# Half of a linear-attention merge on GpSimd, two small copies on ScalarE, and a head's mean one step later

## The chip, the cores and the metric

One core of a Trainium2 chip runs the whole program. The metric is the device time of one execution in microseconds; the kernel before was timed three times (2321.75, 2323.82 and 2325.22 us), and its median is 2323.82 us.

## What is computed

The reference is a two-layer encoder trunk over 16 meta tokens and 256 grid tokens (D = 2048), all in float32. Each layer projects the stream once, runs a gated linear attention (GLA, 4 heads, both directions) and a neighbourhood attention (NA, 16 heads) on parts of that projection, projects the concatenated outputs, normalises, and runs a squared-ReLU MLP. Cut to what matters here, one direction of the GLA is:

```python
bcum = jnp.cumsum(gi, axis=-2)
inter = jnp.einsum('bhtd,bhde->bhte', qi * jnp.exp(bcum), S)
decay = jnp.exp(jnp.where(incl, diff, -jnp.inf))
scores = jnp.einsum('bhtd,bhsd,bhtsd->bhts', qi, ki, decay)
intra = jnp.einsum('bhts,bhse->bhte', scores, vi)
...
o = o * lax.rsqrt(jnp.mean(jnp.square(o), axis=-1, keepdims=True) + LN_EPS) * norm_w
o = o.reshape(B, L, GLA_HEADS * GLA_DV) * jax.nn.silu(r)
```

The last two lines are where a head's mean comes in: a head's output is divided by its root mean square over 256 channels.

## The kernel before

**Weights.** The weights, 770 tiles of 512 KB, stream from HBM once, as 128x1024 tiles (`raw`, issued by SyncE at L195). Each tile is split by `halves` into a high part `wh`, a float32r copy made by ScalarE (ACT, L218), and a low part `wl` = raw - wh made by VectorE (DVE, L219). TensorE (PE) multiplies by both: a dense layer's output is high times high, high times low and low times high, accumulated in PSUM. `raw`, `wh` and `wl` have three buffers each (`wst`, bufs=3). One tile feeds 24 matmuls of 128x272 (L253), or 8 of width 512 and 8 of 256 where the two high terms go as one.

**Order of the work.** The program is written in the order of PE's dense products. After each weight tile `pump` runs steps of two queues of Python generators: `fg` (neighbourhood attention, evictions) and `bg` (the GLA heads). A step is what stands between two `yield`s. `pump` gives `fg` one step and `bg` 1.3 or 1.4 steps a tile (`GLA_R`, `GLA_NA`); a step after `yield True` is one that wants PE, and is held back for up to two tiles until it can go beside another such step. Before the last group of projections of a layer (`g == 5` in `layer`) what is left of `bg` is run to its end at one place. Within this order the recording layer may still move instructions of an engine past each other; each engine then works through its own list in order.

**A GLA head** (`gla_head`, L586 on) has these steps. Decays and the scaled keys and queries lie in `S`: `S[:, 0]` the keys' half, `S[:, 1]` the queries'. Seven levels of a tree double a block at each level: `gather` copies both into `U` (ACT, L606), `merge` multiplies one half of the blocks by the decay total of the neighbouring block, once for the keys' half (`odd` = 0) and once for the queries' (`odd` = 1) (DVE, L615), and then joins the totals in `dec` (GpSimd, called POOL, L617). `group` makes the level scores on PE (L629) and copies them into `A` and `Am` (L641 to L656). PE multiplies across the halves (L681, L686); ACT copies to `A` and `Am` (L692, L696); `stack` and `split` make float32r pairs `am` (L345, L346) and `parts` (L339, L340). The products with V follow (L716 to L720), then squares (ACT, L721), the gate (DVE, L723), their sum `rs` (`grs` in the profile, DVE, L725), the mean, and a Newton step for the inverse root (`newton`, L574 to L578), after which the outputs `y` are split.

**The mean** (`mean`, L975 on) splits `rs` into a pair `sp` (ACT L339, DVE L340), yields, and lets PE sum over the partitions by a matrix of ones (two matmuls, L983). The layer norms use the same helper, without a pool of their own.

**Keys and values of the neighbourhood attention** (`ev_na`): ACT copies the grid columns of a projection out of PSUM (L540), DVE the 16 meta columns, doubled, into a 128x32 strip (L541), POOL two overlaps (L544). Both copies read the PSUM bank `mm` that PE fills again four products later.

## Time and profile before

| what | value |
|---|---|
| median of three runs | 2323.82 us |
| the profiled execution: its own time / its span | 2323.91 us / 2322.1 us |
| PE busy | 2304.2 us (99%) |
| DVE busy | 1526.4 us (66%) |
| ACT busy | 1223.0 us (53%) |
| POOL busy | 155.4 us (7%) |
| mean granted TensorE clock | 0.999 |

The span runs from the first to the last instruction; the execution's own time is 1.8 us longer. Busy time of PE counts matmuls whose ends are modelled, so the places where PE stands still are read from its waits and from the order of time. The merges lie in two stretches, from 108 to about 280 us in layer 0 and from 1293 to 1459 us in layer 1; neighbourhood attention overlaps them, and its last products (L851) start at 1531 us in layer 1.

### The profile page before, as it was taken

How to read it: one execution, taken by the hardware profiler on the slowest of the kernel's cores; microseconds unless marked ns; L12 is line 12 of the kernel's file. 1: busy time of each engine (PE TensorE's matmuls, PEld its weight loads, DVE VectorE, ACT ScalarE, POOL GpSimd, SP SyncE). 2: the span in 40 equal slices, each digit the busy share in tenths (PEclk: the TensorE clock that was granted, in tenths of full speed). 3: DMA queues.
4: the chain of work that ended last, by engine and by line, in shares of the span. 5: the costliest groups of instructions: out<-in, count | busy, mean ns of one | idle time of the engine just before them, and what ended most of it. 6: DMA issues, size and time to landing. Idle time of an engine off the chain costs nothing.

```text
span 2322.1 us, 45272 instructions
## 1 busy us (share of the span) xinstructions
PE 2304.2 (99%) x18420; PEld 2188.9 (94%) x18420; DVE 1526.4 (66%) x2408; ACT 1223.0 (53%) x2096; POOL 155.4 (7%) x232
## 2 busy tenths in 40 slices
PE   9999999999999999999999999999999999999998
PEld 9999999999999999999999899889988888888888
DVE  5588878875544455547576788688866555666655
ACT  5666655564433344444456766655654334555443
POOL 0023210100000000000020122200100000000000
PEclk9999999999999999999999999999999999999999
DMA  8556666565555556665655556665666666667664
GB/s 259 155 164 184 199 189 177 173 181 181 182 181 178 179 181 182 180 179 178 182 173 173 173 175 209 195 187 181 198 191 196 194 191 193 192 196 218 195 195 150
DMA packets 129824, 431.65 MB, mean 186 GB/s; under 512 B 14792, under 2 KB 23496, under 8 KB 129616
## 3 DMA queue, kind: packets, MB, share of 16 engines
q1 hardware_dynamic: 127024, 421.95, 59.9%
q10 hardware_dynamic: 2592, 6.82, 0.8%
q8 instruction: 144, 2.36, 0.4%
q14 instruction: 64, 0.52, 0.1%
HBM read 420.32 MB, written 8.39 MB: 185 GB/s over the span
## 4 chain that ended last, share of the span: by engine, by line
PE 91%; DVE 5%; ACT 2%; issue 1%; DMA 1%; POOL 0%; DVEq 0%; ACTq 0%; SPq 0%
PE mm L253 53%; PE mm L265 29%; PE mm L304 4%; PE mm L314 2%; DVE wl L219 1%; PE bg L304 1%; ACT wh L218 1%; ACT ns L756 0%; DVE S L615 0%; PE bg L851 0%; PE bg L470 0%; PE bg L629 0%; DVE acc L1085 0%; POOL dec L617 0%; DMA raw<-in_wff 0%
## 5 line engine op out<-in xcount | busy, mean ns | idle before, releaser
L219 DVE TENSOR_TENSOR wl<-raw,wh 128x1024 fp32r<-128x1024 f32 (+1 forms) x770 | 935.9, 1223 | 621.8 <-ACT wh L218 518.5
L218 ACT CAST wh<-raw 128x1024 fp32r<-128x1024 f32 (+1 forms) x770 | 804.7, 1047 | 755.8 <-PE mm L253 352.6
L253 PE MATMUL mm<-x,wh 128*128 128x272 f32 (+3 forms) x4544 | 806.8, 294 | 0.0
L253 PEld LDWEIGHTS mm<-x,wh 128*128 128x128 f32 x4544 | 648.0, 188 | 15.5 <-issue 0.8
L253 PE MATMUL mm<-x,wl 128*128 128x272 f32 (+3 forms) x2432 | 520.6, 285 | 2.9 <-DVE wl L219 2.9
L253 PEld LDWEIGHTS mm<-x,wl 128*128 128x128 f32 x2432 | 391.4, 188 | 3.4 <-DVE wl L219 3.4
L253 PE MATMUL mm<-y,wh 128*128 128x272 f32 (+1 forms) x1440 | 235.0, 285 | 0.0
L253 PEld LDWEIGHTS mm<-y,wh 128*128 128x128 f32 x1440 | 199.7, 188 | 0.1
L265 PE MATMUL mm<-x,wh 128*128 128x512 f32 x832 | 193.8, 390 | 0.0
L265 PEld LDWEIGHTS mm<-x,wh 128*128 128x128 f32 x832 | 154.3, 188 | 31.0
L253 PE MATMUL mm<-u,wh 128*128 128x272 f32 (+1 forms) x1056 | 172.1, 285 | 0.0
L265 PE MATMUL mm<-y,wh 128*128 128x512 f32 x688 | 162.3, 389 | 0.0
L265 PEld LDWEIGHTS mm<-y,wh 128*128 128x128 f32 x688 | 128.7, 188 | 26.8 <-issue 0.4
L253 PE MATMUL mm<-y,wl 128*128 128x272 f32 (+1 forms) x720 | 146.5, 284 | 0.0
L253 PEld LDWEIGHTS mm<-u,wh 128*128 128x128 f32 x1056 | 146.3, 188 | 0.0
L265 PE MATMUL mm<-u,wh 128*128 128x512 f32 x496 | 118.3, 391 | 0.0
L253 PEld LDWEIGHTS mm<-y,wl 128*128 128x128 f32 x720 | 112.5, 188 | 0.0
L265 PEld LDWEIGHTS mm<-u,wh 128*128 128x128 f32 x496 | 90.9, 188 | 17.6
L253 PE MATMUL mm<-u,wl 128*128 128x272 f32 (+1 forms) x528 | 107.4, 284 | 0.0
L265 PEld LDWEIGHTS mm<-x,wl 128*128 128x128 f32 x832 | 98.5, 188 | 2.1
L265 PE MATMUL mm<-x,wl 128*128 128x256 f32 x832 | 99.0, 276 | 0.0
L265 PEld LDWEIGHTS mm<-y,wl 128*128 128x128 f32 x688 | 84.3, 188 | 2.8
(275 smaller groups left out, 2285.0 us busy)
## 6 DMA issues: line engine op xcount, KB each, us to landing
raw<-in_wff SPq DMA_DIRECT2D x512, 512.0 KB, 3.6
raw<-in_win SPq DMA_DIRECT2D x190, 512.0 KB, 4.2
raw<-in_wout SPq DMA_DIRECT2D x64, 512.0 KB, 3.9
hop<-nt ACTq DMA_DIRECT2D x16, 384.0 KB, 2.3
np<-hop SPq DMA_DIRECT2D x64, 96.0 KB, 4.1
nb<-in_nab SPq DMA_DIRECT2D x16, 352.0 KB, 4.4
xraw<-in_xT SPq DMA_DIRECT2D x7, 272.0 KB, 5.8
out<-out SPq DMA_DIRECT2D x5, 256.0 KB, 3.1
```

Source lines behind the costliest of these rows:

```text
L218: self.nc.scalar.copy(h, r)
L219: self.wl = self.nc.vector.tensor_tensor(lo, r, h.bitcast(F32), ALU.subtract).ins
L253: mm(o, lhsT=self.block(w, j), rhs=rhs, start=first and not i, stop=last and i == len(TURNS[once]) - 1)
L265: self.nc.tensor.matmul(o, lhsT=self.block(both[j // 8][low], j % 8), rhs=rhs, start=first and not i + j, stop=bool(last and i and j == 15 ...
L304: self.nc.tensor.matmul(ps[g + m][:, :n], lhsT=self.block(parts[p][0], 4 * j + m if first else 2 * m + j), rhs=acts[k + j][parts[p][1]][:, ...
L314: self.nc.tensor.matmul(o, lhsT=self.block(both[low], i), rhs=rhs, start=not low and k + i % 2 == 0, stop=k == DC - 2 and i % 2 == 1 and n ...
```

## The change

Three edits. The meta columns of keys and values are copied by ACT. The keys' half of each merge goes to POOL, the queries' half stays on DVE. And the mean of a GLA head (the one that is given a pool) yields once more between its split and its matmuls, so that a head has one more step.

```diff
-        nc.vector.tensor_copy(rest[:, :, 32:NK2], ps[:, None, T:L].to_broadcast([P, 2, NM]))
+        nc.scalar.copy(rest[:, :, 32:NK2], ps[:, None, T:L].to_broadcast([P, 2, NM]))
...
             for odd in (0, 1):
                 o = blocks(lv, odd, w)
-                tt(o, o, totals(lv, odd, w), ALU.mult)
+                (nc.vector if odd else nc.gpsimd).tensor_tensor(o, o, totals(lv, odd, w), ALU.mult)
...
         self.split(src, *parts)
+        if pool:
+            yield
         yield True
```

From the mean of the first head on, the steps of later heads fall after other tiles than before. Line numbers from L979 on grow by two: the mean's matmuls are L985 after the change.

**ScalarE, last GLA head of layer 0.** Here ACT carries scores from PSUM to `parts`, which the products with V read. Before, four exponentials of the softmax (L756) stand inside the chain:

```order
L540 COPY nv_2205<-mm 128x256
L861 COPY no<-bg 128x272
L339 CAST y_3560<-no 128x2x4x32
L339 CAST y_3560<-no 128x16
L692 COPY A<-bg 128x2x128
L756 ACTIVATE ns,nst<-ns,nst 128x176 x4
L649 COPY near<-bg 128x2x32
L653 COPY A<-bg 64x2x64 x2
L656 COPY A<-near 32x2x64 x4
L696 COPY Am<-bg 16x64 x4
L339 CAST parts<-A 128x544
L345 CAST am<-Am 16x272 x2
```

After the change:

```order
L811 COPY v_4411<-bg 128x256
L692 COPY A<-bg 128x2x128
L649 COPY near<-bg 128x2x32
L653 COPY A<-bg 64x2x64 x2
L656 COPY A<-near 32x2x64 x4
L696 COPY Am<-bg 16x64 x4
L339 CAST parts<-A 128x544
L345 CAST am<-Am 16x272 x2
L540 COPY nk<-mm 128x2x128
L541 COPY nk<-mm 128x2x16
L218 CAST wh<-raw 128x1024
L721 ACTIVATE grs<-bg 128x272
```

The softmax is out of the chain, a meta copy (L541) stands on ACT, and the squares (L721) follow the chain with one weight tile between.

**TensorE, the same head.** Before, the products with V stand whole, 72 dense matmuls behind the last score product (L690):

```order
L253 MATMUL mm<-x_350,wl 128x272
L253 MATMUL mm<-x_353,wl 128x272
L805 MATMUL bg<-ident,nv_2205 128x128 x2
L806 MATMUL bg<-ident,nr_2206 128x128
L808 MATMUL bg<-ident,nms_2218 128x128
L716 MATMUL bg<-parts,V 128x272
L717 MATMUL bg<-parts,V 128x272
L718 MATMUL bg<-parts,y_94 128x272
```

After, 24 dense matmuls (one weight tile) behind it, and four of the next tile in between:

```order
L253 MATMUL mm<-x_622,wl 128x272
L253 MATMUL mm<-x_625,wl 128x272
L716 MATMUL bg<-parts,V 128x272 x2
L253 MATMUL mm<-x_132,wh 128x272 x2
L253 MATMUL mm<-x_133,wh 128x272 x2
L717 MATMUL bg<-parts,V 128x272
L718 MATMUL bg<-parts,y_94 128x272
L716 MATMUL bg<-parts,V 128x272
```

The last head comes three weight tiles later and is finished at the same place as before, where the queue is run to its end. The distance shrank from three tiles to one. In layer 1 there are now 27 dense matmuls in between. From the last product with V to the mean's first matmul there were 24 dense matmuls in both layers; there are 20 now in layer 0 and 15 in layer 1. On DVE the `wl` of three weight tiles stood between that head's splits (L340, L346) and its gate products (L723) in both layers; one stands there now.

**VectorE, a burst between two weight tiles in layer 1.** The rows stand between one `wl` and the next. Before (the piece ahead of the transposes):

```order
L541 COPY nr_16660<-mm 128x2x16
L862 TENSOR_TENSOR no<-no,bg 128x256
L787 TENSOR_TENSOR ns<-mm,nb 128x352 x2
L340 TENSOR_TENSOR y_17544<-no,y_17544 128x2x4x32
L754 TENSOR_REDUCE nst<-ns 128x4
L645 COPY_PREDICATED near<-mask,bg 128x2x32
L615 TENSOR_TENSOR S<-S,dec_14743 128x2x17x8
L645 COPY_PREDICATED near<-mask,bg 128x2x32
L615 TENSOR_TENSOR S<-S,dec_14743 128x2x17x8
L645 COPY_PREDICATED near<-mask,bg 128x2x32
L757 RECIPROCAL nst<-nst 128x4
L615 TENSOR_TENSOR S<-S,dec_14743 128x2x8x16 x2
```

After, at the same weight tile:

```order
L862 TENSOR_TENSOR no<-no,bg 128x256
L787 TENSOR_TENSOR ns<-mm,nb 128x352 x2
L340 TENSOR_TENSOR y_17492<-no,y_17492 128x2x4x32
L754 TENSOR_REDUCE nst<-ns 128x4
L576 SCALAR_TENSOR_TENSOR gtn<-bg,eps,grs 128x256
L615 TENSOR_TENSOR S<-S,dec_14743 128x2x68x2
L577 SCALAR_TENSOR_TENSOR gtn<-gtn,grs 128x256
L578 SCALAR_TENSOR_TENSOR grs<-gtn,grs 128x256
L732 SCALAR_TENSOR_TENSOR on<-on,vec,grs 128x256
L757 RECIPROCAL nst<-nst 128x4
L732 SCALAR_TENSOR_TENSOR on<-on,vec,grs 128x256
L615 TENSOR_TENSOR S<-S,dec_14743 128x2x34x4
```

Six merges and three masked copies stood in this burst; two merges remain, and the third head's Newton step (L576 to L578), its scaling (L732) and the split of its two outputs have moved in. On GpSimd the softmax's product `ns` (L760) stands right ahead of the keys' half of the level of `128x2x34x4`. On SyncE's queue a bias transfer (`nb`, L768) moves by a place or two among the weight tiles.

## The prediction before the run

> **What bounds the kernel now.** I read the page first, for the engine that fills the span.

> ```profile
> span 2322.1 us, 45272 instructions
> PE 2304.2 (99%) x18420; PEld 2188.9 (94%) x18420; DVE 1526.4 (66%) x2408; ACT 1223.0 (53%) x2096; POOL 155.4 (7%) x232
> ```

> PE stands idle for 2322.1 - 2304.2 = 17.9 us of the span, and the change removes no matmul. So whatever it brings or takes must be a wait of PE, or TensorE clock lost behind one. DVE's and ACT's totals matter only where they end such a wait. The view of waits, for PE alone, lists who ends them (total, times, longest):

> ```profile
> PE bg L983 <- ACT sp L339: 3.3, 3, 1.2
> PE mm L253 <- DVE wl L219: 2.9, 2, 2.3
> ...
> PE mm L314 <- DVE nr L541: 0.9, 1, 0.9
> PE mm L304 <- DVE nr L541: 0.8, 1, 0.8
> PE mm L304 <- DVE nms L789: 0.8, 1, 0.8
> ```

> The three edits aim at these rows: the late mean at the first, DVE's load at the second, the meta copies at the third and fourth. Together the four rows hold 3.3 + 2.9 + 0.9 + 0.8 = 7.9 us, 0.34% of the span, which bounds the plain gain. The edits can also make new waits, so I took each place in the order of time.

> **The late mean, first head.** One of the three mean waits belongs to the first head of layer 1:

> ```profile
> 1329.23 0.40 ACT L339 CAST sp<-grs 128x256 fp32r<-128x256 f32 x1 [1.74 <-DVE grs L725]
> ...
> 1329.69 0.38 PE L983 MATMUL bg<-sp,onesr 128*128 128x256 f32 x1 [1.22 <-ACT sp L339]
> ```

> One step more puts half a product, over 2.5 us of dense matmuls, between split and mean. That covers 1.22 us: **-1.2 us**, and nothing queued behind it needs the mean at once.

> **The last head of each layer.** The other two mean waits belong to the last heads, whose remaining steps run at one place before the last projections. The four heads' extra steps delay the last one by three weight tiles, and the place stays. So its products with V now come 24 (layer 0) or 27 dense matmuls (layer 1) after its scores, instead of 72 and more. What has to happen in between stands in the order of time of layer 1:

> ```profile
> 1470.16 0.23 PE L686 MATMUL bg<-X,S 128*32 128x64 f32 x2
> ...
> 1470.52 0.36 ACT L692 COPY A<-bg 128x256 f32<-128x256 f32 x1
> ...
> 1473.98 0.19 ACT L649 COPY near<-bg 128x64 f32<-128x64 f32 x1
> 1474.07 0.53 ACT L653 COPY A<-bg 64x128 f32<-64x128 f32 x2
> ...
> 1474.61 1.22 ACT L656 COPY A<-near 32x128 f32<-32x128 f32 x4
> ...
> 1475.85 0.85 ACT L696 COPY Am<-bg 16x64 f32<-16x64 f32 x4
> ...
> 1476.73 0.62 ACT L339 CAST parts<-A 128x512 fp32r<-128x512 f32 x1
> ...
> 1476.75 0.66 PE L253 MATMUL mm<-x,wh 128*128 128x272 f32 x4
> ...
> 1477.26 0.83 ACT L345 CAST am<-Am 16x256 fp32r<-16x256 f32 x2
> ...
> 1477.51 0.66 PE L253 MATMUL mm<-x,wh 128*128 128x272 f32 x4
> ```

> ACT's copies sum to 0.36 + 0.19 + 0.53 + 1.22 + 0.85 + 0.62 = 3.8 us, about 4.0 with the handovers; in layer 1 the `am` copies (0.83) now stand ahead of `parts`, which makes 4.8. Six dense matmuls take 1477.51 - 1476.75 = 0.76 us, so 24 take 3.0 and 27 take 3.4. PE waits 4.0 - 3.0 = 1.0 and 4.8 - 3.4 = 1.4 us where it did not wait. It can be more: in these rows `parts` ended 1477.35 - 1470.39 = 7.0 us after the scores, with exponentials in between. The bounds are 0.4 and 7.0 - 3.0 = 4.0 us a layer; I take the bare sums, since in the new order no softmax stands inside ACT's chain.

> The means behind them also wait, but less. Layer 0 now:

> ```profile
> 301.11 2.36 DVE L219 TENSOR_TENSOR wl<-raw,wh 128x1024 fp32r<-128x1024 f32 x2
> ...
> 303.95 0.79 DVE L723 TENSOR_TENSOR on<-bg,gate 128x272 f32<-128x272 f32 x2
> ...
> 305.59 0.87 PE L983 MATMUL bg<-sp,onesr 128*128 128x272 f32 x2 [1.13 <-ACT sp L339]
> ```

> The gate products stood behind `wl` work; of three tiles' splits there one stays (minus 2.4 us), while PE's cover shrinks from 24 matmuls to 20 and 15 (0.5 and 1.1 us less) and starts only after the new wait. I put 0.7 us in layer 0 and 0.4 in layer 1 in place of 1.13 and of the third wait, 3.3 - 1.22 - 1.13 = 0.95. So the ends cost 1.0 - 0.4 = **+0.6** and 1.4 - 0.5 = **+0.9 us**.

> **The long DVE burst of layer 1.** The longest `wl` wait, 2.3 us, comes here:

> ```profile
> 1447.86 0.17 DVE L541 COPY nr<-mm 128x32 f32<-128x32 f32 x1
> ...
> 1452.97 1.55 DVE L615 TENSOR_TENSOR S<-S,dec 128x256 f32<-128x256 f32 x2 [0.49 <-ACT U L606]
> ...
> 1456.10 1.23 DVE L219 TENSOR_TENSOR wl<-raw,wh 128x1024 fp32r<-128x1024 f32 x1
> ```

> ```profile
> 1457.39 0.52 PE L253 MATMUL mm<-x,wl 128*128 128x272 f32 x2 [2.32 <-DVE wl L219]
> ```

> ```profile
> 1458.00:1462.00 4.00, 4.00 (x23) 4.00 (x22) 3.24 (x6) 2.31 (x4) 0.33 (x1) 0.59 0.70 173
> ```

> From 1447.9 to 1456.1 DVE makes no `wl`, and PE outruns its three buffers. The window row shows the second part of the price: over the 4 us after it the granted clock is 0.59, a loss of 4.0 x 0.41 = 1.6 us, so this place costs 3.9 us. Behind the 1.13 us of layer 0 it stayed full (the column ahead of the last two):

> ```profile
> 306.00:310.00 4.00, 3.93 (x32) 3.93 (x33) 3.39 (x8) 2.38 (x5) 1.14 (x2) 1.00 0.55 195
> ```

> In the new order the burst at the same tile holds a Newton step, two scalings and two splits in place of four merges and three masked copies, and the merge of the third level waits for POOL, which has the softmax's product ahead of its own half. At 0.43 to 0.48 us a row for what came and 0.43 and 0.21 for what went, the burst is not shorter. I put **+0.5 us** here, from -3.9 (all gone) to +3.

> **Half the merges on POOL.** 56 of 112 go.

> ```profile
> L615 DVE TENSOR_TENSOR S<-S,dec x112: 362/426/1278, 108.1 to 1457.9; 128x272 f32<-128x272 f32 x64, 128x256 f32<-128x256 f32 x48
> ```

> ```profile
> L617 POOL TENSOR_TENSOR dec<-dec x56: 216/462/2857, 108.7 to 1458.1; 128x272 f32<-128x272 f32 x8, 128x136 f32<-128x136 f32 x8, 128x68 f32<-128x68 f32 x8, 128x34 f32<-128x34 f32 x8
> ```

> DVE's list loses 56 x 0.43 = 24 us. POOL shows no such merge; its nearest row is the join of totals at the same size, which stands beside a DVE merge:

> ```profile
> 1439.37 0.75 POOL L617 TENSOR_TENSOR dec<-dec 128x272 f32<-128x272 f32 x1 [7.43 <-DVE S L615]
> ```

> ```profile
> 1439.54 0.88 DVE L615 TENSOR_TENSOR S<-S,dec 128x272 f32<-128x272 f32 x1
> ```

> I take 0.75 us; the bounds are 0.43, DVE's own, and 2.86, the longest join. While POOL ran (to 1440.12), the DVE merge took 0.88 instead of 0.43: it stood until POOL was done. Both halves are released by the same gather, so 0.75 + 0.43 in turn replaces 2 x 0.43, and a `wl` that meets POOL stands too. DVE's 12 us a layer are thus partly given back: by 56 x (0.75 - 0.43) = 18 us in all if every merge meets a DVE product. The gather behind it holds up ACT by at most as much per level, which ACT's waits for free buffers hide. Elsewhere such bursts leave little slack: the other `wl` wait is 2.9 - 2.3 = 0.6 us, in layer 0. I put **+0.5 us** for them, from -0.6 to +2.

> [...]

> **Meta copies on ACT.** 32 copies of 0.18 us leave DVE; on ACT the nearest row, L649 above, is 0.19. At the end of layer 0 they look like a gain:

> ```profile
> 335.14 0.18 DVE L541 COPY nr<-mm 128x32 f32<-128x32 f32 x1
> ...
> 335.38 0.77 PE L304 MATMUL mm<-y,wh 128*128 128x272 f32 x4 [0.83 <-DVE nr L541]
> ...
> 337.15 0.19 DVE L789 TENSOR_TENSOR nms<-mm,qmask 16x48 f32<-16x48 f32 x1
> ...
> 337.48 0.74 PE L304 MATMUL mm<-y,wh 128*128 128x272 f32 x4 [0.83 <-DVE nms L789]
> ```

> PE would start 0.8 us sooner at 335.38, and then stand that much longer for L789, the next in DVE's list. Only the copy's own 0.1 to 0.2 us on DVE is won: **-0.3 us** for both layers, from 0 to -1.7.

> **The sum.** -1.2 + 0.6 + 0.9 + 0.5 + 0.5 - 0.3 = +1.0 us. The profiled execution's own time is 2323.91 us, 0.1 above the median of 2323.82, and so the forecast is **2324.9 us**, no change that can be told: about 0.2% (4.6 us) is what a measurement of this kernel tells from none.

> **Rivals.** (1) *Faster: DVE's relief reaches the burst.* If POOL's halves seldom meet DVE, the burst of layer 1 ends in time: 3.9 us back instead of 0.5 lost, and the 0.6 too. 2324.9 - 4.4 - 1.1 = 2319.4; with short waits at the ends (0.4 each, 1.6 less), 2317.8. For it: six rows of merges become two there. Against: the Newton step and the splits that moved in, and the 0.88 us row.

> (2) *Slower: the last heads starve PE.* If ACT's chain at the ends takes the 7.0 us that it takes now, PE waits 4.0 and 3.6 us for `parts`, and loses clock behind each as it did behind 2.3 us: 2324.9 + (3.0 + 2.2) + 2 x 1.6 = 2333.3. It decides from a chain of about 3.2 + 2.3 = 5.5 us on. One end alone, or a wait of 2 us with a half clock, gives 2328 to 2330.

> (3) *Slower by the port*: if POOL's merges meet DVE as often as they can, by the rows 18 us of standing, the bursts of both layers each stretch by two or three merges, 1.5 to 2 us, and one more wait crosses 2.3 us: 2324.9 + 3.5 + 1.6 = 2330. [...]

> **Chances and range.** The forecast 0.52; rival 1 0.13; rival 2 and its milder forms 0.20; rival 3 0.15. The range 2318.8 to 2333.0 takes in most of each; the forecast's own is 2321 to 2328. Part of the rivals' milder forms lies within 0.2%, so: faster 0.13, same 0.56, slower 0.31.

> **What would show it.** Right: no wait at the first head's mean of layer 1; a new wait of PE for ACT `parts` (L339) at the end of each layer of 1.0 to 1.4 us; a `wl` wait near 1455 us of over 2 us with a low clock behind; POOL merges of 0.7 us and more beside DVE merges over 0.8. Wrong: no `wl` wait over 1 us (rival 1), or waits for `parts` over 2.3 us (rival 2).

## The result, and the profile after

The kernel after the change takes **2339.69 us** (median of 6 runs, 2338.50 to 2341.83) against 2323.15 us (6 runs, 2321.75 to 2325.22) before: 1.0074 times the time, 95% interval 1.0063 to 1.0085, or 16.5 us more. The forecast was 2324.9 us with a range from 2318.8 to 2333.0. It was wrong, and to the slow side. (The ratio is taken over all the runs, so it can differ a little from the quotient of the two medians, here and in the tables below.) The profiled execution's own time is 2339.02 us. Its page begins:

```profile
span 2337.2 us, 45335 instructions
...
PE 2312.5 (99%) x18420; PEld 2195.9 (94%) x18420; DVE 1514.9 (65%) x2320; ACT 1227.3 (53%) x2128; POOL 207.6 (9%) x288
```

The span grew by 15.1 us. DVE is less busy by only 11.5 us, though merges of about 24 us and copies of 32 x 0.18 = 5.8 us left its list, and POOL is busier by 52 us. PE's busy time grew by 8.3 us with the same 18420 matmuls. They took longer, which is lost clock for the most part (mean granted clock 0.996, before 0.999). PE's waits (total, times, longest):

```profile
PE bg L716 <- ACT parts L339: 5.4, 2, 3.0
PE mm L253 <- DVE wl L219: 4.0, 3, 2.0
PE mm L304 <- DVE nms L789: 2.1, 1, 2.1
PE bg L808 <- DVE nms L760: 1.3, 1, 1.3
PE mm L314 <- DVE ns L787: 1.3, 1, 1.3
...
PE mm L304 <- ACT nr L541: 0.7, 1, 0.7
...
PE mm L314 <- ACT nr L541: 0.6, 1, 0.6
```

The mean's row (3.3 us before) is gone, as meant. In its place stands `parts` with 5.4; the `wl` row grew from 2.9 to 4.0; the waits for scores at the ends of the attention stages (`nms` and `ns`, L787 to L789) grew from 0.8 to 3.4, while those for the meta copies (`nr`) fell from 1.7 to 1.3. The clock column (third from the right) shows the rest:

```profile
310.60:314.00 3.40, 3.40 (x17) 3.40 (x16) 1.91 (x3) 2.10 (x5) 0.36 (x2) 0.50 0.00 0
344.80:351.60 6.80, 5.94 (x26) 5.97 (x27) 4.23 (x12) 3.29 (x14) 0.01 (x1) 0.50 0.33 95
1495.10:1498.50 3.40, 3.14 (x14) 3.14 (x15) 1.92 (x2) 1.73 (x5) 0.48 (x2) 0.50 0.00 0
1529.20:1532.60 3.40, 3.40 (x14) 2.98 (x14) 1.66 (x4) 2.04 (x7) 0.00 (x0) 0.50 0.42 142
```

Between the first and the last few microseconds of the program there are five stretches of 3.4 us at half clock (the second row holds two), and they stand behind waits. Before there was one, behind 1458 us. Each costs up to 1.7 us, the four new ones up to 6.8.

To place the loss I compared the start of every dense matmul with the start of the same one before (all 15776 are in both traces; of each 24 in a row the smallest difference, so that a moved head product does not count):

| stretch (us of before) | what is there | us added |
|---|---|---|
| 0 to 204 | projections, first three heads of layer 0 | 0.0 |
| 204 to 290 | last head's merges beside neighbourhood attention, layer 0 | 3.0 |
| 290 to 309 | last head finished | 4.1 |
| 309 to 342 | end of the attention, start of the output projection | 3.2 |
| 342 to 1441 | MLP, layer 1 up to its long burst | 0.2 |
| 1441 to 1461 | the long DVE burst | -1.1 |
| 1461 to 1491 | last head finished | 3.5 |
| 1491 to 1520 | end of the attention, start of the output projection | 2.6 |
| 1520 to the end | | -0.3 |

The sum is 15.2 us. A head product that moved across the boundary of a row shifts about 1 us between neighbouring rows, so single rows are rough. Most of the places are those of the prediction, and the long burst costs 1.1 us less than before. But the last head's merges in layer 0, both ends of the heads and both ends of the attention cost 2.6 to 4.1 us each.

### The profile page after: what moved, and what is told of

The parts are those of the page before. It is cut to its first block, busy times and chain, and to the rows that moved or that the text cites. A ratio compares the mean times of both kernels' runs of the same rounds, so it can differ in the third digit from the quotient of the medians.

```text
span 2337.2 us, 45335 instructions
## 1 busy us (share of the span) xinstructions
PE 2312.5 (99%) x18420; PEld 2195.9 (94%) x18420; DVE 1514.9 (65%) x2320; ACT 1227.3 (53%) x2128; POOL 207.6 (9%) x288
## 3 DMA queue, kind: packets, MB, share of 16 engines
q8 instruction: 144, 2.36, 0.4%
## 5 line engine op out<-in xcount | busy, mean ns | idle before, releaser
L219 DVE TENSOR_TENSOR wl<-raw,wh 128x1024 fp32r<-128x1024 f32 (+1 forms) x770 | 936.6, 1223 | 630.1 <-ACT wh L218 528.7
L218 ACT CAST wh<-raw 128x1024 fp32r<-128x1024 f32 (+1 forms) x770 | 805.0, 1047 | 742.1 <-PE mm L253 356.1
L253 PE MATMUL mm<-x,wh 128*128 128x272 f32 (+3 forms) x4544 | 806.9, 294 | 0.5 <-ACT ft L505 0.5
L253 PEld LDWEIGHTS mm<-x,wh 128*128 128x128 f32 x4544 | 647.7, 188 | 16.5 <-issue 1.0
L253 PE MATMUL mm<-x,wl 128*128 128x272 f32 (+3 forms) x2432 | 521.1, 285 | 4.2 <-DVE wl L219 4.0
L253 PEld LDWEIGHTS mm<-x,wl 128*128 128x128 f32 x2432 | 391.1, 188 | 5.8 <-DVE wl L219 5.7
L253 PE MATMUL mm<-y,wh 128*128 128x272 f32 (+1 forms) x1440 | 235.0, 285 | 0.0
L253 PEld LDWEIGHTS mm<-y,wh 128*128 128x128 f32 x1440 | 199.8, 188 | 0.1
L253 PE MATMUL mm<-u,wh 128*128 128x272 f32 (+1 forms) x1056 | 172.1, 285 | 0.0
L253 PE MATMUL mm<-y,wl 128*128 128x272 f32 (+1 forms) x720 | 146.4, 284 | 0.0
L253 PEld LDWEIGHTS mm<-u,wh 128*128 128x128 f32 x1056 | 146.3, 188 | 0.0
L253 PEld LDWEIGHTS mm<-y,wl 128*128 128x128 f32 x720 | 112.6, 188 | 0.0
L265 PEld LDWEIGHTS mm<-u,wh 128*128 128x128 f32 x496 | 90.9, 188 | 17.6
L253 PE MATMUL mm<-u,wl 128*128 128x272 f32 (+1 forms) x528 | 107.3, 284 | 0.0
```

The source lines that it names most:

```text
L218: self.nc.scalar.copy(h, r)
L219: self.wl = self.nc.vector.tensor_tensor(lo, r, h.bitcast(F32), ALU.subtract).ins
L253: mm(o, lhsT=self.block(w, j), rhs=rhs, start=first and not i, stop=last and i == len(TURNS[once]) - 1)
L265: self.nc.tensor.matmul(o, lhsT=self.block(both[j // 8][low], j % 8), rhs=rhs, start=first and not i + j, stop=bool(last and i and j == 15 ...
```

## Experiments: each edit alone

| run | median us | before on the same chip | ratio, 95% interval |
|---|---|---|---|
| e1: edit 3 alone (late mean) | 2328.20 | 2322.93 | 1.0019 (1.0011 to 1.0028) |
| e2: edits 1 and 2 | 2336.57 | 2322.93 | 1.0057 (1.0045 to 1.0070) |
| e3: edit 2 alone (GpSimd) | 2328.38 | 2322.93 | 1.0026 (1.0016 to 1.0036) |
| e4: edit 1 alone (meta copies) | 2329.84 | 2322.93 | 1.0030 (1.0018 to 1.0041) |

```diff
 # e1: of the change, only
+        if pool:
+            yield
 # e3: of the change, only
-                tt(o, o, totals(lv, odd, w), ALU.mult)
+                (nc.vector if odd else nc.gpsimd).tensor_tensor(o, o, totals(lv, odd, w), ALU.mult)
 # e4: of the change, only; e2 is e3 and e4 together
-        nc.vector.tensor_copy(rest[:, :, 32:NK2], ps[:, None, T:L].to_broadcast([P, 2, NM]))
+        nc.scalar.copy(rest[:, :, 32:NK2], ps[:, None, T:L].to_broadcast([P, 2, NM]))
```

> The late mean alone (third edit), merges and meta copies as before. Theory 1 (the extra steps push the last head of each layer against the place where its queue is run out, PE waits there for ScalarE's parts and loses clock, and the work behind it is late too): 12 to 17 us slower than before, waits of PE for parts (L339) of 2 us and more in both layers. Theory 2 (POOL's merges hold VectorE up): at most 5 us slower, since no merge is on POOL.

> The whole change without the late mean. Theory 1: within 3 us of before, no wait for parts at the ends of the stages. Theory 2: 8 to 15 us slower than before, with VectorE's weight splits late.

> Keys' half of the merges on POOL alone. Theory 1: within 3 us of before; VectorE's remaining merges last longer than 0.43 us where POOL's run, but what they lose is hidden. Theory 2: 8 to 15 us slower.

> Meta copies on ScalarE alone. Both theories: within 2 us of before; the two waits of PE for the meta copy at the ends of the layers stay or turn into waits for VectorE's scores.

Both theories missed the sizes: e1 is at 5.3 us where theory 1 had 12 to 17 and theory 2 at most 5, e3 at 5.5 between its two bands, and e4 at 6.9 where both had at most 2. Only e2, at 13.6 us, fell into a band, that of theory 2, whose ground was the merges alone. Theory 1's sign was there in e1 all the same, the wait for `parts` at the ends of both layers:

```profile
PE bg L716 <- ACT parts L339: 4.9, 2, 2.8
```

No edit carries the loss. Alone they cost 5.3, 5.5 and 6.9 us, 17.6 together against 16.5 measured for all three. So each needed an explanation of its own.

## Experiments on edit 3: how late the last head is

In the kernel after, the last head of layer 0 ends like this (PE's last score products run from 303.98 to 304.21; ACT carries the scores to `parts`):

```profile
304.05 1.21 DVE L219 TENSOR_TENSOR wl<-raw,wh 128x1024 fp32r<-128x1024 f32 x1
...
304.27 0.37 ACT L692 COPY A<-bg 128x256 f32<-128x256 f32 x1 [0.76 <-PE bg L690]
...
305.76 0.50 DVE L645 COPY_PREDICATED near<-mask,bg 128x64 f32<-128x64 uint8 x2
...
306.29 0.21 ACT L649 COPY near<-bg 128x64 f32<-128x64 f32 x1 [1.65 <-DVE near L645]
...
306.94 1.22 ACT L656 COPY A<-near 32x128 f32<-32x128 f32 x4
...
308.19 0.85 ACT L696 COPY Am<-bg 16x64 f32<-16x64 f32 x4
309.06 0.64 ACT L339 CAST parts<-A 128x544 fp32r<-128x544 f32 x1
...
309.76 0.52 PE L716 MATMUL bg<-parts,V 128*128 128x272 f32 x2 [2.38 <-ACT parts L339]
```

From the scores to `parts` 309.70 - 304.21 = 5.5 us pass, not the 4.0 of ACT's copies alone: ACT stands 1.65 us for DVE's masked copies (L645), which in DVE's list stand behind a `wl`. PE's wait of 2.38 us and the half clock behind it (up to 1.7) are the cost here. The mean's wait of 1.13 us, which stood in this stretch before, is gone. In layer 1 PE's last score product ends at 1488.84:

```profile
1490.22 0.38 ACT L692 COPY A<-bg 128x256 f32<-128x256 f32 x1
...
1491.95 0.21 ACT L649 COPY near<-bg 128x64 f32<-128x64 f32 x1 [0.61 <-DVE near L645]
...
1494.69 0.62 ACT L339 CAST parts<-A 128x512 fp32r<-128x512 f32 x1
...
1495.36 0.80 PE L716 MATMUL bg<-parts,V 128*128 128x256 f32 x2 [2.98 <-ACT parts L339]
```

Two ways of having the last head in time again, and a control:

```diff
 # e5: the whole change; e7: edit 3 alone; both without the yield behind the split into parts
-        yield
         yield True
         while 2 * h + 1 not in self.gate:
 # e6: the whole change; e12: edit 3 alone; e11: the kernel before; each with
-GLA_R, GLA_NA, NORMS = 1.3, 1.4, (1.0, 0.6)
+GLA_R, GLA_NA, NORMS = 1.3, 1.6, (1.0, 0.6)
```

> The whole change, but the yield right behind the split into parts is taken out, so that a head has as many steps as before and the last head of each layer comes as early as before: its products with V again stand 72 and 70 dense matmuls behind its scores. Beside the kernel before, dense matmul for dense matmul, the whole change lost about 3.2 us at 306 us (last head, layer 0) and about 3 us at 1488 us (last head, layer 1). Theory A (edit 3 costs what it does because the last head comes three weight tiles later): these two steps go, 2339.7 - 6.4 = about 2333 us, PE's waits for parts fall from 5.4 us to under 0.5, and one or two half-clock stretches of 3.4 us go with them. Theory B (a later mean and the lists that it reorders cost it, wherever the last head stands): 2337 us or more.

> The kernel before with the late mean alone, and without the yield behind the split into parts: as many steps a head as before. Theory A: the last heads are in time, so nothing of the 5.3 us of edit 3 is lost; the wait of the first mean of layer 1 (1.2 us) goes, those of the last heads stay: 2322 to 2323 us, mean waits 2.1 us. Theory B: 2326 us or more, as with edit 3 alone.

> The whole change, with 1.6 steps of the queue of heads for a weight tile in neighbourhood attention in place of 1.4 (GLA_NA). The last head of each layer is then finished long before the place where the queue is run to its end: its products with V stand 72 dense matmuls behind its scores, and its mean 72 and 70 behind them. Theory A (of the change's loss, what edit 3 adds is the last head's lateness): no waits for parts and none for the means, 2339.7 - 3.4 (what the run without the extra step gave back) - 2.2 (the means it still waited for) = about 2334 us. Theory B (a higher rate packs the merges closer, and DVE's bursts cost as much as the lateness did): 2337 us or more.

> The kernel before, with GLA_NA 1.6 in place of 1.4 and nothing else. The last head is finished earlier, and its mean stands 72 and 70 dense matmuls behind its last product with V instead of 24. Theory A (a mean's wait is a matter of distance only): the two mean waits of the last heads go (2.1 us), that of the first head of layer 1 stays (1.2): 2321 us. Theory B (the merges packed closer lengthen DVE's bursts): 2324 us or more.

> The kernel before with edit 3 alone and GLA_NA 1.6: every head's products with V stand 5.6 us of dense matmuls or more behind its scores, and every mean as far behind them. Theory A: all three mean waits go (3.3 us) and no wait for parts comes: about 2320 us, 8 us less than edit 3 without the rate. Theory B: the bursts take it back, 2324 us or more.

| run | median us | before on the same chip | ratio, 95% interval |
|---|---|---|---|
| e5: whole change, as many steps as before | 2336.30 | 2323.27 | 1.0059 (1.0046 to 1.0071) |
| e7: late mean, as many steps as before | 2322.84 | 2323.27 | 0.9999 (0.9990 to 1.0007) |
| e6: whole change, rate 1.6 | 2330.73 | 2323.31 | 1.0034 (1.0022 to 1.0046) |
| e11: before, rate 1.6 | 2323.11 | 2323.31 | 1.0002 (0.9993 to 1.0011) |
| e12: late mean, rate 1.6 | 2322.92 | 2323.31 | 1.0000 (0.9991 to 1.0009) |

With as many steps as before, edit 3 costs nothing, alone (e7) or on top of the others (e5 is at e2's 2336.57). So its price is the last head's lateness. I had expected 2333 of e5, and it lies between its two theories. The waits for `parts` (L716) went as theory A had it, but in e2 and e5, which have no late last head, PE waits 2.2 us for `wh` (L218) in the burst of layer 1 and about 1.9 us for `nms` (L760, in e5 L759) near 281 us, where the whole change has no wait for `wh` and 1.3 us for `nms`. So in the sum edit 3 is worth only the 3.1 us by which e2 is below the whole change. The rate of 1.6 gives back 9 us of the whole change (2339.7 to 2330.7), more than expected; why so much was not worked out.

But the late mean wins nothing either. In e7 (edit 3 with as many steps as before) the mean's row fell from 3.3 to 2.2 us as planned, and another rose from 0.9 to 1.8:

```profile
PE bg L984 <- ACT sp L339: 2.2, 2, 1.2
PE mm L314 <- DVE nr L541: 1.8, 1, 1.8
```

In e12 all three mean waits (3.3 us) and the long `wl` wait are gone, and the median stays. In e11 two of the mean waits are gone, and its median stays as well. The longest rows of e12 are new ones, score products that wait for the gathers (L629) and for the meta scores (L808, L681), presumably since at 1.6 steps a tile the merges follow each other more closely:

```profile
PE bg L629 <- ACT U L606: 2.2, 3, 1.3
PE bg L808 <- DVE nms L760: 1.6, 3, 0.7
...
PE bg L681 <- DVE Am L647: 1.0, 1, 1.0
```

None of e7, e11 and e12 can be told from the kernel before. No version that I ran beats it.

## Experiments on edit 2: where GpSimd's merge is paid for

The groups of merges in the kernel after (shortest, median and longest in ns):

```profile
L615 DVE TENSOR_TENSOR S<-S,dec x56: 377/444/1144, 108.4 to 1474.7; 128x272 f32<-128x272 f32 x32, 128x256 f32<-128x256 f32 x24
L615 POOL TENSOR_TENSOR S<-S,dec x56: 617/876/1947, 108.5 to 1474.8; 128x272 f32<-128x272 f32 x32, 128x256 f32<-128x256 f32 x24
```

GpSimd's median is 0.88 us, where the sum took 0.75. What hangs on it is the next gather, an ACT copy in front of which ACT then stands. The gathers' group before (busy us, mean ns | idle just before them, and what ended it):

```profile
L606 ACT COPY U<-S 128x272 f32<-128x272 f32 (+1 forms) x104 | 40.7, 427 | 24.3 <-DVE S L615 21.5 <-DVE S L660 2.7
```

With edit 2 alone (e3):

```profile
L606 ACT COPY U<-S 128x272 f32<-128x272 f32 (+1 forms) x104 | 40.9, 427 | 38.0 <-DVE S L615 31.4 <-POOL S L615 3.4 <-DVE S L660 2.7
```

ACT stands 13.7 us longer there. Mostly DVE's half is named as the one that came last, although it is the shorter. In e3 in layer 1, on ACT:

```profile
1449.29 0.74 ACT L606 COPY U<-S 128x272 f32<-128x272 f32 x2 [1.27 <-DVE S L615]
1451.29 0.41 ACT L606 COPY U<-S 128x256 f32<-128x256 f32 x1 [1.25 <-DVE S L615]
1451.60 1.05 ACT L218 CAST wh<-raw 128x1024 fp32r<-128x1024 f32 x1
```

on GpSimd,

```profile
1450.17 0.72 POOL L615 TENSOR_TENSOR S<-S,dec 128x272 f32<-128x272 f32 x1 [1.59 <-ACT U L606]
```

on DVE,

```profile
1450.26 0.94 DVE L615 TENSOR_TENSOR S<-S,dec 128x272 f32<-128x272 f32 x1
```

and on PE:

```profile
1459.77 0.77 PE L253 MATMUL mm<-x,wh 128*128 128x272 f32 x4 [2.15 <-ACT wh L218]
...
1461.89 0.41 PE L253 MATMUL mm<-x,wl 128*128 128x272 f32 x1 [1.35 <-DVE wl L219]
```

DVE's merge runs from 1450.26 to 1451.20. It takes 0.94 us, until 0.31 us after the end of GpSimd's at 1450.89. The gather waits for it, and the weight copy `wh` stands behind the gather. The next `wh` stands behind a softmax and two more gathers; PE waits 2.15 us for it and 1.35 for the `wl` made from it, where before one `wl` wait of 2.3 stood. So I gave GpSimd the three earlier heads (e9), the last one alone (e14), and then every merge, but with a product of the same size left in each freed place of DVE's list (e15). In e15 TensorE, DVE and ACT keep the order of before, row for row:

```diff
 # e9; e14 with h < 3 in place of h == 3
+                (nc.vector if odd or h == 3 else nc.gpsimd).tensor_tensor(o, o, totals(lv, odd, w), ALU.mult)
 # e15: z is a scratch tile; VectorE squares the gathered U into it
+                (nc.vector if odd else nc.gpsimd).tensor_tensor(o, o, totals(lv, odd, w), ALU.mult); odd or tt(z[...], u, u, ALU.mult)
```

> Edit 2 alone, for heads 0 to 2 of each layer; the last head, whose merges fall beside neighbourhood attention, keeps both halves on DVE. Beside the kernel before, edit 2 alone lost 1.1 us at 277 us, 1.1 at 339 (a half-clock stretch at another place) and 2.1 at 1454, the first and third of them in the last head's merges. Theory A (a slower merge holds back the gathers, which on ACT stand ahead of the softmax and of wh, where both meet): those go, 2328.4 - 3.5 = about 2325 us or less. Theory B (GpSimd and DVE exclude each other on SBUF wherever a merge meets a DVE product): three quarters of the 5.5 us stay, 2327 us or more.

> Edit 2 for the last head of each layer alone: 14 merges' halves on GpSimd, 42 stay on DVE. Theory A (the whole price of edit 2 is paid where the last head's merges fall beside neighbourhood attention): 2327 us or more, with PE's wait for wh of about 2 us near 1457 us. Theory B (no single place: the three other heads and the last one disturb each other, and neither alone costs much): 2325 us or less.

> Edit 2 alone, and in the place of each half that went to GpSimd VectorE makes a product of the same size into a scratch tile that nobody reads. The order on TensorE, VectorE and ScalarE is then that of before, row for row; what differs is that the gathers hang on GpSimd's merges and that both engines read SBUF at once. Theory A (edit 2's 5.5 us come from the order of VectorE's list, as edit 1's did): 2324.5 us or less. Theory B (GpSimd's merge is slower, and the gathers, ScalarE's wh behind them and VectorE on the shared SBUF pay for it): 2327 us or more, the more as VectorE has its whole load.

| run | median us | before on the same chip | ratio, 95% interval |
|---|---|---|---|
| e9: heads 0 to 2 | 2324.53 | 2323.27 | 1.0006 (0.9997 to 1.0014) |
| e14: last head only | 2326.91 | 2323.68 | 1.0013 (1.0004 to 1.0022) |
| e15: all heads, DVE's list kept full | 2333.09 | 2322.50 | 1.0047 (1.0034 to 1.0061) |

Forty-two of the 56 merges cost 1.3 us, not to be told from nothing; the 14 of the last heads cost 3.2, with a wait of 1.8 us for `wh` at 1457 us. That fits theory A in the main, with e14 just short of its 2327. The two intervals overlap, so that the last heads pay most is likely and not proved. In e15 the order of the lists is unchanged and the loss is 10.6 us, so a changed order is not needed for a loss. The 10.6 us are the price of the merges on GpSimd while DVE keeps its whole load. A part of it may belong to the dummies, which run beside GpSimd's merges themselves (551 ns on the mean, where DVE's merges before take 466). In e3 DVE is spared about 24 us, but its list and ACT's also have another order than before; how the 5.5 us divide between the slower merge, DVE's longer merges beside it (566 ns on the mean in e3, 466 before) and that order was not separated. PE's largest row in e15 is DVE's `wl`, which was 2.9 us before:

```profile
PE mm L253 <- DVE wl L219: 6.5, 6, 3.2
```

## Experiments on edit 1: copies that cost nothing, and a list that changed

Thirty-two meta copies of 0.18 us moved to an engine that is busy 53% of the time, and 6.9 us were lost. PE's waits with edit 1 alone (e4):

```profile
PE bg L808 <- DVE nms L760: 2.5, 3, 1.6
PE mm L304 <- DVE nms L789: 2.1, 1, 2.1
PE mm L253 <- DVE wl L219: 1.7, 1, 1.7
PE mm L314 <- DVE ns L787: 1.3, 1, 1.3
PE mm L253 <- ACT wh L218: 1.2, 1, 1.2
```

Most of what is new here ends at DVE. The profiled spans differ by 5.9 us (2328.0 and 2322.1). About 3 us of that are longer waits of PE, and up to 3.4 are two half-clock stretches more than before (mean granted clock 0.997 and 0.999). At 218 us, in the first pair of neighbourhood attention, DVE's list before:

```profile
209.49 0.51 DVE L787 TENSOR_TENSOR ns<-mm,nb 128x352 f32<-128x352 f32 x1
...
215.46 0.25 DVE L760 TENSOR_TENSOR nms<-nms,mst 16x96 f32<-16x96 f32 x1
```

and with edit 1 alone (e4):

```profile
209.22 1.21 DVE L219 TENSOR_TENSOR wl<-raw,wh 128x1024 fp32r<-128x1024 f32 x1
210.36 0.91 DVE L732 SCALAR_TENSOR_TENSOR on<-on,vec,grs 128x272 f32<-128x272 f32 x2
...
211.70 0.52 DVE L787 TENSOR_TENSOR ns<-mm,nb 128x352 f32<-128x352 f32 x1
...
217.96 0.20 DVE L760 TENSOR_TENSOR nms<-nms,mst 16x96 f32<-16x96 f32 x1
```

A `wl` (L219) now stands ahead of the scaling of a head (L732) and of the scores (L787), and a transpose ahead of the small softmax (L760). All of it comes 2.2 to 2.5 us later, with no copy in sight. PE, which did not stand here before, waits 1.57 us for `nms`, and from 219.6 on the clock is 0.50 for 3.4 us. At the start of the output projection of layer 0 the recording layer likewise puts three sums of the residual (L424) and a weight split ahead of the pair's output (L862); the scores L789 come at 339.68 in place of 337.15. Three runs tell the copies from the list:

```diff
 # e8: edit 1, but the last pair of a layer on VectorE
+        (nc.scalar.copy if j < 21 else nc.vector.tensor_copy)(rest[:, :, 32:NK2], ...)
 # e10: both copy; ScalarE's goes to a scratch tile
+        nc.scalar.copy(scratch, ...); nc.vector.tensor_copy(rest[:, :, 32:NK2], ...)
 # e13: both copy; VectorE's goes to a scratch tile
+        nc.scalar.copy(rest[:, :, 32:NK2], ...); nc.vector.tensor_copy(scratch, ...)
```

> Edit 1 alone, but the last pair of heads of each layer (projections 21 to 23) keeps its meta copies on DVE. Beside the kernel before, edit 1 alone lost about 1.8 us and a half-clock stretch near 218 us, 1.3 us near 339, 0.8 near 1454 and 2.9 near 1516 to 1520 us. Theory A (a meta copy on ACT delays the last pair's output copy and with it the scores at the end of each stage): the losses at 339 and 1516 go, 2329.8 - 4.2 = about 2325.6 us, and PE's waits for nms and ns of L787 to L789 at the ends are back at 0.8 us or less. Theory B (ACT's load as such: each copy makes wh later, in the whole stretch): 2328.5 us or more.

> The kernel before, with each meta copy made twice: by DVE as before, and by ScalarE into a scratch tile that nobody reads. ScalarE has the 32 copies of edit 1, the order of DVE's instructions stays that of before but for one merge. Theory A (edit 1 costs through DVE's list, in which weight splits then stand ahead of the scores and of the softmax of the meta tokens): 2324.5 us or less. Theory B (the copies on ScalarE themselves make wh and the output copies late): 2327 us or more.

> The kernel before, with the meta columns copied by ScalarE into the strips that the scores read, as edit 1 has it, and by DVE into a scratch tile that nobody reads. The order of DVE's and TensorE's instructions is that of before, row for row. Theory A (edit 1's 6.9 us come from the order of DVE's list alone): 2324.5 us or less, and no wait for nms over 1 us at 218 us. Theory B (a strip that comes from ScalarE comes later, and the scores and what stands behind them with it): 2327 us or more.

| run | median us | before on the same chip | ratio, 95% interval |
|---|---|---|---|
| e8: not the last pair | 2328.22 | 2323.27 | 1.0023 (1.0014 to 1.0032) |
| e10: both copy, DVE's counts | 2324.00 | 2323.31 | 1.0005 (0.9996 to 1.0013) |
| e13: both copy, ACT's counts | 2323.79 | 2323.68 | 1.0002 (0.9993 to 1.0011) |

e10 has all 32 copies on ACT beside DVE's and loses nothing that can be told, so their load is not the price. In e13 the strips come from ACT as in edit 1, DVE's instructions and, but for one swap of attention products (L851, L858), PE's stand in the order of before, and nothing is lost. At 218 us PE does not wait, and its one wait for `nms` (L760) is that of before, at 343 us:

```profile
PE bg L808 <- DVE nms L760: 0.7, 1, 0.7
```

So the 6.9 us come with the order that the lists take when 32 small copies are taken out of DVE's. By the waits above it is mostly DVE's own list. In e4 ACT's list has another order too, with gathers and copies moved, and the new wait of 1.2 us for `wh` ends there; e10 and e13 keep both lists, so they do not part the two. e8 lies just below its theory B. At the ends of the attention the waits for `nms` and `ns` are back at 0.8 us, as its theory A had it, but those for the copies (`nr`) grew to 2.6, so that all of them together are 3.4 us in e8, 3.6 in e4 and 2.5 before. The 1.57 us at 218 stay. That e8's profile is 3.8 us shorter than e4's is mostly clock, since e4's has three half-clock stretches and e8's has none (mean granted clock 0.997 and 1.000). Why the recording layer moves weight splits ahead when the copies leave was not examined.

## Why the prediction was wrong, step by step

- **The late mean, first head (-1.2 us): right as far as it went.** The wait is gone after the change. In e7, where nothing else costs, it is gone too, but a wait for a bank at the end of layer 1 is 0.9 us longer, and the time is that of before.
- **The last heads (+0.6 and +0.9): the mechanism right, the size wrong.** The waits for `parts` came where forecast, at 2.4 and 3.0 us instead of 1.0 and 1.4. The step that failed is "I take the bare sums, since in the new order no softmax stands inside ACT's chain": that chain also waits for DVE's masked copies, which stood behind a `wl`, and in layer 1 its first copy started 1.4 us after the scores, behind ACT's other work. It took 5.5 us, and in layer 1 from 1488.84 to 1495.31, 6.5. Rival 2 was to decide from 5.5 us on, and both waits were followed by half clock, as that rival had it.
- **The means behind them (0.7 and 0.4 left): wrong, and of no weight.** None is left: PE now stands for `parts` first, and the rest is covered.
- **The burst of layer 1 (+0.5): the sign wrong.** A `wl` wait of 2.0 us stayed, but no half clock followed it; beside before the place gained 1.1 us. That gain is luck: the half clock that did not come is worth up to 1.7 us, and it turned on where the wait fell (last section).
- **Half the merges on POOL, elsewhere (+0.5): too small by far.** Alone it cost 5.5 us. The step that failed is that the gather "holds up ACT by at most as much per level, which ACT's waits for free buffers hide". Where the last head's merges meet the softmax, the `wh` rows of e3 show no such waits, ACT stands for the merges instead, and PE waits 2.15 us for `wh`. GpSimd's merge took 0.88 us at the median, not the 0.75 of the join.
- **The meta copies (-0.3): wrong in sign, and the largest miss, 6.9 us alone.** "Only the copy's own 0.1 to 0.2 us on DVE is won" takes the rest of the list as fixed. It was not. At the end of layer 0, where PE was known to wait for DVE, the new order could have been read, and there sums and a weight split stood ahead of the scores. The largest single wait that is new, at 218 us, came where PE had not waited at all.
- **The clock.** I charged half clock to the burst alone, since behind 1.13 us it had stayed full (1.00 from 306 to 310 us). The new waits brought it, with 1.9 to 3.0 us of standing at each end of the heads and of the attention: four stretches more, up to 6.8 of the 15.1 us.

Rivals 2 and 3 each had the mechanism of one edit. I priced them as alternatives; they came together, with a third that I had not listed, and the three prices add up to within about 1 us of the whole. Of rival 3 the rows show DVE's merge standing until GpSimd's is done (last section); what the two engines share there, the port of its title, no run shows.

## What to carry to other kernels

Where PE is busy 99% of the time, the lists of the other engines have little slack at a few places, and an edit that spares an engine work can cost more by the order its list then takes than by the work itself: compare the new order at each place where the profile shows a wait, before pricing the instructions, and look for small products that move behind long ones elsewhere too. A step added to a queue that is emptied at a fixed place is paid by the last item in it, so count the distance there and price its chain through every engine that takes part. To tell work from order, leave a dummy of the same size in the old place, and remember that the dummy does work too (e15).

## What the runs showed of the hardware

DVE and GpSimd together: in the kernel after, 20 of DVE's 56 merges started while one of GpSimd's was running, and 18 of them ended 0.28 to 0.30 us after it, as in the rows of e3 at 1450 us (0.31). The other two, of 0.44 and 0.43 us, ended while GpSimd's (1.95 and 1.19 us) still ran. In the kernel before, the five merges that started beside a join of totals (L617) took 0.88 us each and ended 0.30 us after it, where those that met nothing on GpSimd took 0.37 to 0.45. A `wl` that meets GpSimd stands as well: the one that started at 1339.26 us, beside a join that ran from 1339.07 to 1339.65, took 1.46 us, where the median of those that met nothing on GpSimd is 1.23. DVE's merges take 466 ns on the mean before and 566 in e3, while their median hardly moves (426 and 438): the price falls on those that meet GpSimd. This is what the prediction read from its two rows at 1439 us.
